# State transitions and state steps of a chunked RWKV-7 mixer, per pair of heads or per head

## The chip, the cores and the metric

The kernel runs on one core of a Trainium2 chip. The metric is device time in microseconds (us) of one execution; the time before is the median of three runs. TensorE does the matrix products (each as a load of weights, "PEld", and a product, "PE"), VectorE (DVE) and ScalarE (ACT) move and combine tiles, GpSimd (POOL) does some elementwise work and gathers, and SyncE (SP) issues most DMAs. An fp32 product of this kernel appears in the trace as two loads and two products.

## The reference, cut to what matters

Two layers, each a mixer (RWKV-7 time mixing beside a pooling mixer) and a PEER expert feed-forward. 512 tokens, width 1024, 8 RWKV heads of 64. The part that the change touches is the recurrence of each head, whose state is a 64 by 64 matrix:

```python
def rwkv7_step(state, inp):
    r_t, w_t, k_t, v_t, kk_t, a_t = inp
    sa = jnp.einsum('bhvk,bhk->bhv', state, -kk_t)
    state = (state * w_t[:, :, None, :]
             + sa[..., None] * (kk_t * a_t)[:, :, None, :]
             + v_t[..., None] * k_t[:, :, None, :])
    y = jnp.einsum('bhvk,bhk->bhv', state, r_t)
    return state, y
```

## The kernel before, in words

The mixer cuts the 512 tokens into 16 chunks of 32 (`CH`) and works on four pairs of heads per layer. Inside a pair the two heads lie one above the other on the 128 partitions (`hrs[0]` is rows 0 to 63, `hrs[1]` rows 64 to 127). Within a chunk everything is made by products; from chunk to chunk a state `M` of 128 x 64 (both heads) is carried: `M(c+1) = diag(P_c) M(c) + G_c^T M(c) + H_c`.

For each pair a list of blocks is written out: scaled and transposed copies, Gram matrices (`gram`, L625 and L628), `wu` (products L644, copies L646 and L572 on ScalarE), `hmat(0)`, `gmat`, `hmat(1)` and two `ypart`. `gmat` makes the 16 transitions: for each of 4 groups of 128 tokens and each of the 4 chunks in it one product of 32 rows and 128 columns (L662), into four PSUM banks, one per chunk position. Since both heads are in one product, the two off-diagonal 64 x 64 blocks mix the heads and are wrong; VectorE copies each bank (128 x 512) out and multiplies it with the mask `bones` of two diagonal blocks (L665). `hmat` (L674, copied by ScalarE at L678) makes the additive parts, in products of 64 x 64.

`chain(c)` is a state step: one product of 128 x 128 with the 64 columns of `M` (L706) into the single bank of the pool `psc`, and two operations of VectorE on 128 x 64: `M * P + H` (L707) and the sum with the product (L708). Step c needs `M` of step c-1. Step 0 is a copy, so there are 14 products per pair, 112 in all. `yout` (L717) applies the states in 64 x 64 products and `gn1`, `gn2` (L724 to L745) normalise.

The lists of different pairs are zipped: the later blocks of pair p go with the steps of pair p-1, the first blocks of pair p+2, the `adaLN` projections (DMA `raw<-ada`, VectorE L195 and L197) and, later, fills of the output projection (L277). The framework then orders each engine's instructions in a plan of its own, which follows the order of the program as a priority and its own estimate of when operands, tiles and banks are ready. Every engine runs its list in order. PSUM has eight banks: five in pool `ps`, two in `pss`, one in `psc`; a bank is taken again when its reader is done. SBUF tiles of 128 x 512 come from one pool, `s2`, of 38 slots.

Of the kernel before, what the change touches and what calls it, by code (L numbers as in the profile page):

```python
# [14 lines left out]
AF = mybir.ActivationFunctionType  # L15
ALU = mybir.AluOpType
# [3 lines left out]
P = 128  # L20
T = 512
NT = T // P
# [3 lines left out]
CH = 32  # L26
# [82 lines left out]
def body(ctx, tc, A, tap=None):  # L109
    nc = tc.nc  # L110
    V, S, G, TE = nc.vector, nc.scalar, nc.gpsimd, nc.tensor
# [11 lines left out]
    def nm(p):  # L123
        cnt[0] += 1
        return f"{p}{cnt[0]}"
# [6 lines left out]
    def sbank(shape=(P, T)):  # L132
        return pss.tile(list(shape), F32, tag="pss", name=nm("pss"))

    def s2t(name, shape=(P, T), dt=F32):
        return s2.tile(list(shape), dt, tag="s2", name=nm(name))
# [12 lines left out]
    def C(n):  # L149
        o, w = COFF[n]  # L150
        return const[:, o:o + w]
# [166 lines left out]
    def mixer(l):  # L318
        with ExitStack() as mctx:
# [126 lines left out]
            for p in range(4):  # L446
# [7 lines left out]
                for h in range(2):  # L454
                    hd = 2 * p + h
                    for cc in range(4):
                        rows = slice(cc * CH, (cc + 1) * CH)
# [4 lines left out]
                if p % 2 == 1:  # L462
                    for cc in range(4):
                        rows = slice(cc * CH, (cc + 1) * CH)
# [103 lines left out]
            def bank2(shape=(P, T)):  # L568
                nb[0] += 1
                return sbank(shape) if nb[0] % 4 == 0 and not apart[0] else psp[0].tile(list(shape), F32, tag="ps", name=nm("ps"))  # L570
# [4 lines left out]
            def pair(p):  # L575
                at, bt, kt, rt, v = at_[p], bt_[p], kt_[p], rt_[p], v_[p]
                hrs = [slice(h * 64, (h + 1) * 64) for h in range(2)]
                q3 = lambda n: s2t(n, (P, NT, P))
                z = {}
# [74 lines left out]
                def W(t):  # L654
                    return z["WU", t // 2][:, t % 2].rearrange("p h c -> p (h c)")[:, 64:192]

                def gmat():
                    pgs = [bank2((P, NT, P)) for _ in range(4)]
                    for t in range(NT):
                        for cc in range(4):  # L660
                            rows = slice(cc * CH, (cc + 1) * CH)
                            TE.matmul(pgs[cc][:, t], W(t)[rows], z["bk", cc % 2][rows, t], start=True, stop=True, tile_position=(cc * CH, 0))  # L662
                    for cc in range(4):
                        z["G", cc] = q3("G")
                        V.tensor_tensor(z["G", cc], pgs[cc], C("bones").unsqueeze(1).to_broadcast([P, NT, P]), op=ALU.mult)  # L665

                def hmat(s):
                    def f():
# [12 lines left out]
                def ypart(h):  # L681
                    def f():
# [3 lines left out]
                        for t in range(NT):  # L686
# [6 lines left out]
                blocks = [scaled(0, bt), scaled(1, kt), swapped, transposed("vT", v), gram("ak", kt, at, "lt"),  # L693
                          transposed("AX", at), transposed("UV", None), transposed(("bk", 0), None), transposed(("bk", 1), None), xm(0), xm(1),
                          gram("rb", bt, rt, "le"), gram("rkm", kt, rt, "le"), wu(0), wu(1), hmat(0), gmat, hmat(1), ypart(0), ypart(1)]

                def chain(c):
                    def f():
                        if c == 0:
                            z["M"] = [s2t("M", (P, 8, 64)) for _ in range(2)]  # L700
                            S.activation(z["M"][0][:, 1], z["H", 0][:, 0, 0], AF.Copy)
                            return
                        M = lambda i: z["M"][i // 8][:, i % 8]
                        hc = z["H", (c % 4) // 2][:, c % 2, c // 4]
                        pm = psc.tile([P, 64], F32, tag="psc", name=nm("psc"))
                        TE.matmul(pm, z["G", c % 4][:, c // 4], M(c), start=True, stop=True)  # L706
                        V.scalar_tensor_tensor(hc, M(c), PC[:, p, c:c + 1], hc, op0=ALU.mult, op1=ALU.add)  # L707
                        V.tensor_tensor(M(c + 1), hc, pm, op=ALU.add)  # L708
                    return f
# [605 lines left out]
```

## Time and profile before

| | us |
|---|---|
| median of 3 runs | 3448.68 |
| lowest and highest of these | 3448.21, 3457.46 |
| profiled execution, its own time | 3438.13 |
| its span, first to last instruction | 3436.4 |

Views of a profile give start and duration in us from the start of the span. "Idle before" an instruction is followed by an arrow to what ended the wait. In a table of stretches each engine has its busy time and, in brackets, its number of instructions; PEclk is the granted clock of TensorE as a share of 2.4 GHz.

### The profile page before, as it was taken

The numbers are of one execution on the slowest core, as the hardware profiler recorded it, in microseconds if no ns is written. First come the engines' busy times: TensorE is split into PE (matmuls) and PEld (weight loads), VectorE is DVE, ScalarE is ACT, GpSimd is POOL, SyncE is SP. The second block draws the span as 40 slices with busy tenths as digits, with TensorE's granted clock in tenths as the row PEclk, the third lists the DMA queues.
The fourth block names the chain that finished last, engine by engine and source line by source line (L and its number), as shares of the span: only waits on it lengthen the run. The fifth ranks groups of instructions, "written<-read, shape, count | busy, mean of one in ns | idle before, by whom it ended". The sixth has DMA issues, their size and how long they took to land. (4 is left out here: it accounts for less than half of the span.)

```text
span 3436.4 us, 51106 instructions
## 1 busy us (share of the span) xinstructions
PE 3211.2 (93%) x18154; PEld 2814.1 (82%) x18154; DVE 2809.3 (82%) x6227; ACT 1386.0 (40%) x2228; POOL 875.7 (25%) x684
## 2 busy tenths in 40 slices
PE   5889888999999999999899898999999999999997
PEld 3777678999998888888777777889999888888886
DVE  5677499989868888899939675999997688888998
ACT  3433222446563334333353323334656533333333
POOL 2000001432202222555500000023240122245564
PEclk7989899999999999999999888999999999999998
DMA  5214253567789999999922233345767999999996
GB/s 196 77 47 144 88 176 122 171 228 257 262 310 344 345 343 342 350 377 398 356 72 82 79 111 117 99 134 180 275 237 282 333 334 343 342 340 335 362 392 237
DMA packets 361377, 826.41 MB, mean 240 GB/s; under 512 B 46496, under 2 KB 189600, under 8 KB 357792
## 3 DMA queue, kind: packets, MB, share of 16 engines
q1 hardware_dynamic: 287392, 554.68, 47.5%
q0 software_dynamic: 73728, 268.47, 20.8%
q8 instruction: 142, 2.33, 0.3%
q14 instruction: 115, 0.94, 0.1%
HBM read 730.75 MB, written 92.27 MB: 240 GB/s over the span
## 5 line engine op out<-in xcount | busy, mean ns | idle before, releaser
L277 PE MATMUL pss<-hi,wsp 128*128 128x384 f32 (+1 forms) x5168 | 1081.5, 360 | 88.4 <-DVE wsp L260 27.8
L1162 PE MATMUL ps<-vv,wg 128*128 128x512 f32 x4608 | 1077.3, 392 | 22.7 <-DVE vv L1146 6.9
L277 PEld LDWEIGHTS pss<-hi,wsp 128*128 128x128 f32 x5168 | 941.0, 195 | 162.8 <-DVE wsp L260 39.9
L1162 PEld LDWEIGHTS ps<-vv,wg 128*128 128x128 f32 x4608 | 866.0, 189 | 208.0 <-ACT vv L1145 10.4
L259 ACT ACTIVATE wsp<-raw 128x1024 fp32r<-128x1024 f32 x341 | 360.0, 1057 | 548.5 <-PE pss L277 428.9
L277 PE MATMUL pss<-lo,wsp 128*128 128x384 f32 (+1 forms) x2584 | 534.1, 347 | 0.0
L855 POOL DMA_INDIRECT row<-u,ex x256 | 318.8, 1245 | 837.1 <-DVE row L861 639.5
L260 DVE TENSOR_TENSOR wsp<-raw,wsp 128x1024 fp32r<-128x1024 f32 x341 | 432.4, 1269 | 69.9 <-ACT wsp L259 69.7
L277 PEld LDWEIGHTS pss<-lo,wsp 128*128 128x128 f32 x2584 | 461.4, 188 | 22.2 <-issue 0.5
L855 POOL DMA_INDIRECT row<-v,ex x256 | 336.3, 1314 | 244.5 <-DVE ox L869 190.6
L1146 DVE TENSOR_TENSOR vv<-raw,vv 128x512 fp32r<-128x512 f32 x512 | 345.4, 692 | 43.1 <-ACT vv L1145 39.3
L1145 ACT ACTIVATE vv<-raw 128x512 fp32r<-128x512 f32 x512 | 291.4, 619 | 111.5 <-DMA raw<-v 76.9
L1136 ACT ACTIVATE wg<-ge 128x384 fp32r<-128x384 f32 x256 | 132.9, 524 | 497.6 <-DVE ge L1134 206.3
L861 DVE SCALAR_TENSOR_TENSOR row<-row,hx 128x1024 f32<-128x1024 f32 x256 | 318.4, 1250 | 14.0 <-DMA row<-u,ex 14.0
L869 DVE SCALAR_TENSOR_TENSOR ox<-row,wx,ox 128x1024 f32<-128x1024 f32 x254 | 325.3, 1281 | 2.4
L971 POOL TENSOR_TENSOR eq<-eq,cid 128x400 f32<-128x400 f32 x128 | 181.7, 1439 | 478.8 <-DVE eq L969 341.1
L937 POOL TENSOR_TENSOR hf<-hi,lo 128x128 f32<-128x128 f32 x16 | 7.8, 503 | 925.6 <-DVE tw L906 450.4
L1137 DVE TENSOR_TENSOR wg<-ge,wg 128x384 fp32r<-128x384 f32 x256 | 141.3, 555 | 104.6 <-ACT wg L1136 93.9
L1046 ACT ACTIVATE gb<-ps 128x512 f32<-128x512 f32 x192 | 199.0, 1161 | 0.0
L1134 DVE TENSOR_TENSOR ge<-ge,g 128x192 f32<-128x192 f32 x496 | 157.0, 353 | 46.3 <-DMA g<-gscr 39.3
L1129 ACT ACTIVATE ge<-pss 128x384 f32<-128x384 f32 x80 | 39.2, 490 | 249.0 <-PE pss L277 243.1
L1025 DVE TENSOR_TENSOR oh<-oh,selg 128x1024 f16<-128x1024 f16 x96 | 71.2, 742 | 44.9 <-PE ps L1044 44.7
(459 smaller groups left out, 3194.5 us busy)
## 6 DMA issues: line engine op xcount, KB each, us to landing
raw<-uT SPq DMA_DIRECT2D x256, 512.0 KB
raw<-v SPq DMA_DIRECT2D x256, 512.0 KB
gscr<-gb SPq DMA_DIRECT2D x24, 2048.0 KB
g<-gscr SPq DMA_DIRECT2D x124, 384.0 KB
gespill<-ge SPq DMA_DIRECT2D x176, 192.0 KB
ge<-gespill SPq DMA_DIRECT2D x176, 192.0 KB
ada<-ada SPq DMA_DIRECT2D x96, 256.0 KB
raw<-ada SPq DMA_DIRECT2D x48, 512.0 KB
```

What stands on the lines that cost most here:

```text
L259: S.activation(w[:, 0], raw, AF.Copy)
L260: V.tensor_tensor(w[:, 1], raw, w[:, 0].bitcast(F32), op=ALU.subtract)
L277: TE.matmul(pt, w[:, a, k * P:(k + 1) * P], hs[k][b], start=start and n == 0, stop=stop and n == len(steps) - 1)
L855: G.indirect_dma_start(out=rows[n], out_offset=None, in_=A["u" if n < P else "v"], in_offset=bass.IndirectOffsetOnAxis(ap=ex[:, n % P:n % ...
L861: V.scalar_tensor_tensor(row, row, 1.0, hx, op0=ALU.mult, op1=ALU.mult, accum_out=dots[:, e:e + 1])
L869: V.scalar_tensor_tensor(ox, row, wx[:, e:e + 1], ox, op0=ALU.mult, op1=ALU.add)
L971: pace["G"] = G.tensor_tensor(eq, eq, z["id"][:, h].unsqueeze(1).to_broadcast([P, 8, NC]), op=ALU.mult)
L1046: S.activation(gb[:, :, o:o + 4].rearrange("p i t -> p t i"), pt, AF.Copy, scale=1.0 / GSC)
L1134: V.tensor_tensor(gq, gq, g[:, :, c % IG], op=ALU.mult)
L1145: S.activation(vv[0][q], raw[:, q * T:(q + 1) * T], AF.Copy)
L1146: vlo[q] = V.tensor_tensor(vv[1][q], raw[:, q * T:(q + 1) * T], vv[0][q].bitcast(F32), op=ALU.subtract)
L1162: end[0] = TE.matmul(acc[t][d2], wg[a][:, ts_], vv[b][d2], start=(c == 0 and a == 0 and b == 0), stop=(c == NK - 1 and a == 1))
```

## The change

The transitions are made per head: 32 products of 32 rows and 64 columns per pair instead of 16 of 128 columns, each head into its own half of the partitions. The result holds no block that mixes heads, so there is no mask: ScalarE copies 128 x 256 out of each bank where VectorE multiplied 128 x 512, and two tiles hold what four held. A state step takes two products of 64 rows and 64 columns, one per head, into the two halves of the same bank.

```diff
                 def gmat():
-                    pgs = [bank2((P, NT, P)) for _ in range(4)]
+                    pgs = [bank2((P, NT, 64)) for _ in range(4)]
                     for t in range(NT):
                         for cc in range(4):
                             rows = slice(cc * CH, (cc + 1) * CH)
-                            TE.matmul(pgs[cc][:, t], W(t)[rows], z["bk", cc % 2][rows, t], start=True, stop=True, tile_position=(cc * CH, 0))
+                            for h in range(2):
+                                TE.matmul(pgs[cc][hrs[h], t], W(t)[rows, hrs[h]], z["bk", cc % 2][rows, t, hrs[h]], start=True, stop=True, tile_position=(cc * CH, h * 64))
                     for cc in range(4):
-                        z["G", cc] = q3("G")
-                        V.tensor_tensor(z["G", cc], pgs[cc], C("bones").unsqueeze(1).to_broadcast([P, NT, P]), op=ALU.mult)
+                        if cc % 2 == 0:
+                            z["G", cc // 2] = s2t("G", (P, 2, NT, 64))
+                        S.activation(z["G", cc // 2][:, cc % 2], pgs[cc], AF.Copy)
...
-                        TE.matmul(pm, z["G", c % 4][:, c // 4], M(c), start=True, stop=True)
+                        for h in range(2):
+                            TE.matmul(pm[hrs[h]], z["G", (c % 4) // 2][hrs[h], c % 2, c // 4], M(c)[hrs[h]], start=True, stop=True)
```

## Rows read from the trace of the kernel before

**Rows 1.** The page's first lines: span, and busy time of each engine.
```profile
span 3436.4 us, 51106 instructions
PE 3211.2 (93%) x18154; PEld 2814.1 (82%) x18154; DVE 2809.3 (82%) x6227; ACT 1386.0 (40%) x2228; POOL 875.7 (25%) x684
```
**Rows 2.** Table of stretches, three in each layer's mixer: start:end, length, busy by engine, clock.
```profile
250.60:256.00 5.40, 4.46 (x17) 3.50 (x16) 3.60 (x11) 0.00 (x0) 0.00 (x0) 0.50 0.01 3
284.90:291.40 6.50, 5.25 (x19) 3.32 (x17) 4.95 (x14) 0.00 (x0) 0.00 (x0) 0.64 0.00 1
329.10:336.60 7.50, 6.00 (x29) 4.53 (x28) 5.69 (x16) 0.63 (x1) 0.00 (x0) 0.86 0.00 0
...
1947.60:1953.00 5.40, 4.46 (x17) 3.50 (x16) 3.58 (x11) 0.00 (x0) 0.00 (x0) 0.50 0.00 0
1987.50:1993.20 5.70, 4.51 (x22) 2.79 (x15) 4.70 (x13) 0.00 (x0) 0.00 (x0) 0.71 0.00 1
2029.70:2037.00 7.30, 5.75 (x27) 3.99 (x26) 5.64 (x17) 0.63 (x1) 0.00 (x0) 0.82 0.01 2
```
**Rows 3.** Timeline of the second of these stretches, TensorE and then VectorE.
```profile
284.94 0.43 PE L706 MATMUL psc<-M,G 128*128 128x64 f32 x2
288.24 0.69 PE L706 MATMUL psc<-M,G 128*128 128x64 f32 x2 [0.31 <-DVE M L708]
290.53 1.06 PE L602 MATMUL pss<-const,bk 128*128 128x128 f32 x4
...
288.50 0.68 DVE L665 TENSOR_TENSOR G<-ps,const 128x512 f32<-128x512 f32 x1
290.49 0.68 DVE L665 TENSOR_TENSOR G<-pss,const 128x512 f32<-128x512 f32 x1
```
**Rows 4.** Timeline of ScalarE around the first layer's stretches.
```profile
256.18 1.08 ACT L613 ACTIVATE UV<-ps 128x512 f32<-128x512 f32 x2 [6.24 <-PE ps L602]
292.59 0.63 ACT L727 ACTIVATE sq<-y 128x512 f32<-128x512 f32 x1 [9.19 <-DVE y L725]
333.88 0.63 ACT L727 ACTIVATE sq<-y 128x512 f32<-128x512 f32 x1 [9.73 <-DVE y L725]
```
**Rows 5.** Instructions by line, whole span: duration in ns as min/median/max.
```profile
L665 DVE TENSOR_TENSOR G<-ps,const x26: 679/681/693, 230.3 to 2033.8; 128x512 f32<-128x512 f32 x26
L678 ACT ACTIVATE H<-ps x28: 378/383/418, 231.2 to 2039.6; 128x256 f32<-128x256 f32 x28
L706 PEld LDWEIGHTS psc<-M,G x224: 186/189/338, 238.9 to 2074.3; 128*128 128x128 f32 x112
```
**Rows 6.** Timeline of TensorE: weight loads of state steps and of 64 x 64 products.
```profile
342.30 0.30 PEld L706 LDWEIGHTS psc<-M,G 128*128 128x128 f32 x2
342.52 0.30 PEld L687 LDWEIGHTS ps<-rb,WU 128*128 128x128 f32 x2
346.94 1.36 PEld L717 LDWEIGHTS ps<-rt,M 64*64 64x64 f32 x44
348.35 0.30 PEld L706 LDWEIGHTS psc<-M,G 128*128 128x128 f32 x2
348.71 0.54 PEld L717 LDWEIGHTS ps<-rt,M 64*64 64x64 f32 x16
320.29 0.33 PEld L674 LDWEIGHTS ps<-UV,('bk', 0)439_2249 64*64 64x64 f32 x16
246.49 0.74 PEld L662 LDWEIGHTS ps<-('bk', 0)263_1492,WU 32*128 32x128 f32 x8 [0.17 <-issue]
```
**Rows 7.** Timeline: first and last of the 112 state steps, weight loads.
```profile
238.95 0.30 PEld L706 LDWEIGHTS psc<-M,G 128*128 128x128 f32 x2
...
2074.22 0.30 PEld L706 LDWEIGHTS psc<-M,G 128*128 128x128 f32 x2 [0.19 <-DVE M L708]
```
**Rows 8.** Timeline of ScalarE behind the first pair's `gmat`, first layer.
```profile
231.23 0.66 ACT L678 ACTIVATE H<-ps 128x256 f32<-128x256 f32 x2
232.42 0.38 ACT L678 ACTIVATE H<-pss 128x256 f32<-128x256 f32 x1 [0.53 <-PE pss L674]
```

## The prediction

> **What bounds the kernel now.** I read the page's head first. TensorE has something in flight for 93% of the span and its weight loads for 82%; VectorE is busy 82%, ScalarE 40% [rows 1]. So work taken from VectorE is worth nothing by itself: it pays only where TensorE stood still for it. The diff touches two short places, the two mixers (about 220 to 400 us and 1920 to 2100 us), so I cut these into stretches. Three stretches in each layer stand out [rows 2]: ScalarE is idle, VectorE half busy, the granted clock at 0.50 to 0.86, and TensorE holds only 15 to 28 weight loads in 5 to 8 us. Their lengths add up to 5.4 + 6.5 + 7.5 + 5.4 + 5.7 + 7.3 = 37.8 us, and weight loads run in 3.50 + 3.32 + 4.53 + 3.50 + 2.79 + 3.99 = 21.6 us of it.
>
> The timeline of one of them says why [rows 3]. From 284.94 to 288.24 us TensorE does nothing but five state steps one behind the other, each waiting for VectorE's L708 of the step before. The four transition banks had been written just before. VectorE takes them out only from 288.50 to 291.2 us, because its list holds the steps first and it waits inside each of them for TensorE. Until then four of seven banks are full, and the transposes of the next pair (L602) begin in earnest at 290.53. ScalarE stands idle meanwhile, for 6.24, 9.19 and 9.73 us in the first layer's three stretches [rows 4]. So the stretches are a hold: banks wait for a mask, the mask waits behind a chain, and TensorE has only the chain to run.
>
> **The change part by part.** *The copy.* It removes 32 masks (four per pair, eight pairs) of 0.681 us from VectorE, 21.8 us, and adds 32 copies of 128 x 256 from PSUM to ScalarE; the same shape costs 0.383 us at L678 [rows 5], 12.3 us in all. Neither sum is on the path. What is on it is when the banks come free. On ScalarE, idle in these stretches [rows 4], four copies take 4 x 0.383 = 1.5 us and can start as soon as the products are done: in the stretch of [rows 3] they would end near 286.5 instead of 291.2 us. Then transposes, `hmat(1)` and `ypart` fill the gaps between the steps. What can be gained is the time without a weight load, 37.8 - 21.6 = 16.2 us for both layers. I take four fifths, 13 us, since at the head of each stretch a step or two still stands alone. Lower bound: nothing, if the copies come late too. Upper bound: all 16.2, and more if the clock holds: weighted by their lengths it is 0.69 in these stretches [rows 2], and a third of 21.6 us of loads is another 7, so 23 us.
>
> *The steps.* A step's two loads occupy TensorE for 0.22 us in a stream (342.30 to 342.52). Four loads of 64 x 64 on two quarters are shown by `yout`: 44 loads in 1.36 us, that is (1.36 - 0.14) / 43 = 0.028 us each, 0.11 us for a step [rows 6]. So 0.11 us less for each of 112 steps [rows 7]. Some 28 of them lie in the stretches counted above; 84 x 0.11 = 9.2 us remain. `yout` streams 32 columns per product and a step 64, but the loads set the pace in that row. Bounds: nothing, if the two heads don't overlap, and 12.3 us, if all 112 count.
>
> *Changes of shape.* A step that goes from products of 128 rows to `yout`'s quarters starts the next load 0.36 us after its own first one (348.35 to 348.71), against 0.22 us in one shape: 0.14 us for a change [rows 6]. I counted the neighbours of the steps over the timeline between the first and the last [rows 7]. There are 80 uninterrupted groups of steps. 41 begin behind, and 42 end before, products that use a part of the array: 83 changes now. As quarters, steps fit with `yout` and `hmat` (18 of the beginnings, 31 of the ends) and change against all others: 62 + 49 = 111. The difference, 28 x 0.14 = 3.9 us, is lost. Bounds: none, if the order shifts kindly, and 224 - 83 = 141 changes, 19.7 us, if every step comes to stand alone among full products.
>
> *The transition products.* 256 loads of 32 x 128 become 512 of 32 x 64. Before, eight loads on two row groups took 0.74 us, (0.74 - 0.19) / 7 = 0.079 us each; small products on four quarters took (0.33 - 0.14) / 15 = 0.013 us each at L674 [rows 6]. No row shows 32 x 64. Bounds: 512 x 0.028 - 256 x 0.028 = 7 us lost, if each load costs the same whatever its width, and 256 x 0.079 - 512 x 0.013 = 13.6 us gained. I take nothing: half the columns, twice the loads, the same array.
>
> *The first pair of each layer* has no such hold: VectorE was free there, and ScalarE copies `H` from 231.23 and again at 232.42 us [rows 8]. The new copies queue behind the first, delay the second by up to 1.5 us, and keep `hmat(1)`'s successors waiting for banks. I charge 1 us per layer, 2 us (bounds 0 and 3.1). The two saved tiles of `s2` per pair I count as nothing: no wait that I read was for a slot, and adaLN and the copies have slots now; if that cover is gone, it can only help. DMA stays as it is: its share was 0.01 or less in the stretches [rows 2].
>
> *Sum* against the profiled execution of 3438.13 us: -13 - 9.2 + 3.9 + 0 + 2 = -16.3 us. That execution lies 10.5 us under the median of the runs, 3448.68 us; nothing in the sum depends on this, so I carry the difference over: 3432 us.
>
> **The rule that speaks against it.** `yout`'s loads run at 0.028 us though its two heads, rows 0 to 63 and rows 64 to 127, write two halves of one bank [rows 6], just as the new steps do. The Trainium skill, TensorEngine Tiling (Array Packing), section Restrictions and Gotchas, says that different row tiles cannot access the same PSUM bank simultaneously. By that rule the heads of a step would take turns; this trace does not agree. The rival below needs no more than the mechanism.
>
> **Rivals.** *The hold stays* (chance 0.20). ScalarE's list is in order too. In two of the three stretches its next instruction waits for VectorE's `y` (L725) [rows 4]. If the plan puts the copies behind it, or if TensorE's list still holds the steps in a row, the 13 us don't come: -9.2 + 3.9 + 2 = -3.3 us, 3445 us, no measurable change. Against it: the copies stand earlier in the program than those normalisations, and their operands are ready earlier.
>
> *The heads take turns* at the bank (0.05). Four loads of half the columns one after the other cost what two of all columns cost, 0.22 us; the 9.2 us are lost, -7.1 us, 3442 us, still within the measurement. For it is only that no row shows 64 columns per quarter; against it stands the row of `yout`.
>
> *Changes of shape outweigh the rest* (0.13), the slower side. If the hold goes, steps are spread among other products, 128 wide most of them, and each pays 0.14 us on either side. With the 13 us intact it would need (13 + 9.2 - 2) / 0.14 = 144 added changes, as many as there can be. With the hold in place it needs (9.2 - 2) / 0.14 = 51 to reach no change and about 125 to pass 0.3%. At 141 added changes and no relief: 19.7 + 2 - 9.2 = 12.5 us more, 3461 us.
>
> **How the numbers follow.** My forecast, the hold dissolved, has 0.62: 3432 us, and by its own bounds (-23 - 9.2 - 4 for a kind order and narrower transitions, to -4 where a quarter of the hold's gain comes) 3412 to 3444. A measurement of this kernel tells about 0.3%, 10 us, from no change, so faster means under 3438. The forecast's case falls there in nearly all its weight, and the measured fate of the rivals gives: faster 0.62, same 0.27 (both middle rivals and the forecast's weak end), slower 0.11. The range reaches to the two middle rivals and to no change: 3412 to 3450.
>
> **What would show it.** Right: in each mixer the L665 rows of VectorE are gone and ScalarE copies `G` within 2 us of the last L662; groups of four or five steps with waits of 0.31 us shrink to one or two; the three stretches get shorter by 2 us each and their clock rises; a step's loads take 0.11 us in a stream. Wrong: the G copies start late, behind an instruction of ScalarE that waits; or the steps' loads are 0.05 us apart and not overlapped; or gaps of 0.3 us before and after single steps add up to more than 10 us. The prediction falls too if the time saved in the mixers returns as a longer wait for VectorE or for adaLN's DMA before the feed-forward.

## The result, and the profile after

The changed kernel takes 3418.26 us (median of 8 runs, 3415.88 to 3425.93) against 3443.37 us (8 runs, 3433.64 to 3457.46): ratio 0.9928 [0.9912, 0.9945], some 25 us. (Five more runs have lowered the median before from the 3448.68 us that the forecast counted from.) The same pair measured again gave 0.9890 [0.9858, 0.9923], 38 us. Its profiled execution took 3418.91 us. The page's first lines, which answer to [rows 1]:

```profile
span 3417.1 us, 52040 instructions
...
PE 3187.3 (93%) x18634; PEld 2786.5 (82%) x18634; DVE 2787.6 (82%) x6195; ACT 1396.2 (41%) x2260; POOL 867.6 (25%) x684
```

The gain lies in the two mixers. The table of stretches, each mixer from its first `wu` product (L644) to its first update of `x` (L794 before, L797 after), first of the kernel before and then of the changed one (columns as in [rows 2]: busy us and counts of TensorE's products, its weight loads, VectorE, ScalarE, GpSimd; granted clock; DMA share; GB/s):

```profile
225.29:392.48 167.19, 153.15 (x1345) 126.62 (x1344) 107.14 (x255) 50.84 (x115) 0.00 (x0) 0.83 0.26 83
1922.10:2089.05 166.95, 151.13 (x1345) 124.75 (x1344) 107.27 (x255) 50.84 (x115) 0.00 (x0) 0.86 0.26 83
sum 334.14, PE 304.29 PEld 251.37 DVE 214.41 ACT 101.67 POOL 0.00; mean PE 152.14 PEld 125.68 DVE 107.21 ACT 50.84 POOL 0.00
```

```profile
226.32:379.82 153.50, 139.31 (x1585) 112.16 (x1584) 97.03 (x238) 55.48 (x130) 0.00 (x0) 0.88 0.29 90
1916.01:2068.83 152.82, 139.58 (x1585) 111.12 (x1584) 97.18 (x238) 55.42 (x130) 0.00 (x0) 0.87 0.29 91
sum 306.32, PE 278.88 PEld 223.28 DVE 194.21 ACT 110.90 POOL 0.00; mean PE 139.44 PEld 111.64 DVE 97.10 ACT 55.45 POOL 0.00
```

Both mixers together shrink from 334.1 to 306.3 us, 27.8 us, and the weight loads in them from 251.4 to 223.3 us, 28.1 us. The time without a weight load is 334.1 - 251.4 = 82.8 us before and 306.3 - 223.3 = 83.0 us after. So TensorE saves what it loads, and the time without a load comes out the same. That speaks against my largest term, which was a wait; but the same total can hide one wait that grew and one that shrank, and the experiments show that it does.

Outside the mixers the changed kernel's profile is 8.5 us longer (spans less mixers: 3102.3 and 3110.8 us). Two profiles of the kernel before differ there by 15 us (3102.3 and 3117.3), so this shows no loss.

The same stretches behind `gmat` as in [rows 2], each from the last transition products to the first stream of `hmat` or `ypart` behind the transposes, in the changed kernel:

```profile
249.60:252.21 2.61, 1.95 (x21) 1.45 (x21) 2.35 (x8) 1.19 (x4) 0.00 (x0) 1.00 0.00 0
283.20:286.59 3.39, 2.74 (x39) 1.57 (x22) 3.09 (x11) 1.21 (x4) 0.00 (x0) 1.00 0.00 0
324.40:328.90 4.50, 3.65 (x58) 2.47 (x54) 2.60 (x9) 1.40 (x4) 0.00 (x0) 0.95 0.00 0
1939.30:1941.89 2.59, 1.94 (x20) 1.43 (x21) 2.32 (x9) 1.17 (x4) 0.00 (x0) 1.00 0.01 3
1970.70:1973.31 2.61, 2.29 (x19) 1.32 (x18) 2.50 (x8) 1.20 (x4) 0.00 (x0) 1.00 0.00 0
2014.60:2019.35 4.75, 3.90 (x54) 2.73 (x55) 2.84 (x9) 1.39 (x4) 0.00 (x0) 0.86 0.00 0
sum 20.45, PE 16.47 PEld 10.97 DVE 15.69 ACT 7.56 POOL 0.00; mean PE 2.74 PEld 1.83 DVE 2.62 ACT 1.26 POOL 0.00
```

They have shrunk from 37.8 to 20.5 us, by 17.3, of which 6.7 us are time without a load (16.2 to 9.5 us), and the clock in them has risen from 0.50 to 0.86 up to 0.86 to 1.00. (The clock is that of one profile. In the changed kernel's second one the first stretch, from 253.33 to 256.81 us, takes 3.5 us at a clock of 0.72.) Seen by themselves these rows seem to confirm the hold. What ended the first stretch shows in the timelines of pair 1, layer 0. First the kernel before, weight loads and VectorE's first mask:

```profile
250.68 0.50 PEld L706 LDWEIGHTS psc<-M,G 128*128 128x128 f32 x2 [0.22 <-issue]
...
251.68 0.50 PEld L706 LDWEIGHTS psc<-M,G 128*128 128x128 f32 x2 [0.50 <-DVE M L708]
...
252.68 0.50 PEld L706 LDWEIGHTS psc<-M,G 128*128 128x128 f32 x2 [0.50 <-DVE M L708]
...
253.68 0.50 PEld L706 LDWEIGHTS psc<-M,G 128*128 128x128 f32 x2 [0.50 <-DVE M L708]
...
253.95 0.68 DVE L665 TENSOR_TENSOR G<-ps,const 128x512 f32<-128x512 f32 x1
253.95 0.87 PEld L602 LDWEIGHTS pss<-const,bk 128*128 128x128 f32 x4
```

And the changed kernel, ScalarE's copies and weight loads, with the products of one step:

```profile
249.58 0.38 ACT L667 ACTIVATE G<-ps 128x256 f32<-128x256 f32 x1
...
249.61 0.20 PEld L709 LDWEIGHTS psc<-M,G 64*64 64x64 f32 x4 [0.17 <-DVE M L711]
...
249.86 0.38 ACT L667 ACTIVATE G<-pss 128x256 f32<-128x256 f32 x1
...
250.12 0.67 ACT L667 ACTIVATE G<-ps 128x256 f32<-128x256 f32 x2
...
250.26 0.20 PEld L709 LDWEIGHTS psc<-M,G 64*64 64x64 f32 x4 [0.46 <-DVE M L711]
250.27 0.33 PE L709 MATMUL psc<-M,G 64*64 64x64 f32 x4 [0.33 <-DVE M L711]
...
250.92 0.20 PEld L709 LDWEIGHTS psc<-M,G 64*64 64x64 f32 x4 [0.46 <-DVE M L711]
...
251.18 0.42 PEld L602 LDWEIGHTS pss<-const,bk 128*128 128x128 f32 x4
```

Before, the transposes (L602) load at 253.95, 0.27 us behind the last step's load and in the same moment in which the *first* mask begins; no bank of `G` had come free. After, they load at 251.18, again 0.26 us behind the last step. Layer 1 shows the same 0.27 us in both kernels. TensorE's list has four steps of the pair before there (the first of them, after, between the last transition products, at 248.95), and the transposes come next in the list. (Why the plan puts four steps there, and whether it reckons with the banks, no run shows; it did so in every kernel below.) The stretch is so many steps times the period of a step: 1.00 us before, at a clock of 0.50, and 0.655 us after. At the full clock the period before was 0.75 us, in the stretch of [rows 3]:

```profile
285.69 0.30 PEld L706 LDWEIGHTS psc<-M,G 128*128 128x128 f32 x2 [0.45 <-DVE M L708]
...
286.44 0.30 PEld L706 LDWEIGHTS psc<-M,G 128*128 128x128 f32 x2 [0.45 <-DVE M L708]
```

In pair 2 the mean product of the pair before stands between the steps and the transposes, from 288.62 to 289.68 us before and from 284.84 to 285.38 after: the same work at the two levels of the clock.

The steps' weight loads over the whole span, before and after (busy us, mean ns, idle time just before them and what ended it):

```profile
L706 PEld LDWEIGHTS psc<-M,G 128*128 128x128 f32 x224 | 40.3, 220 | 32.5 <-DVE M L708 27.4 <-issue 0.9
```

```profile
L709 PEld LDWEIGHTS psc<-M,G 64*64 64x64 f32 x448 | 24.5, 143 | 32.8 <-DVE M L711 20.0 <-issue 5.0 <-DVE H L710 3.6
```

40.3 us have become 24.5, 15.8 less, while the idle time in front comes out the same (32.5 and 32.8 us). In all fourteen profiles of this document these loads take 38.8 to 41.3 us where the steps are full and 24.3 to 25.8 us where they are narrow. A step's period is its loads plus a wait for VectorE that does not depend on the width: 0.30 + 0.45 = 0.75 us before at full clock, 0.20 + 0.46 = 0.66 us after. The transition products' weight loads in the two mixers (length of the mixers, busy us; mean of one mixer), L662 before and L663 after:

```profile
sum 334.14, PEld 18.30; mean PEld 9.15
```

```profile
sum 306.32, PEld 11.27; mean PEld 5.64
```

Another 7.0 us; 17.9 to 20.5 us with full transitions and 11.1 to 11.4 us with narrow ones in the fourteen profiles. The rest lies in lines that the change does not touch, counted in the same way (loads of different lines can overlap, so the lines do not add up to the whole): the transposes L602 12.4 to 9.2 us, the variance products 12.8 to 10.4, `ypart` 48.6 to 44.3, `yout` 20.1 to 21.1. These are as many loads of the same shapes as before; the granted clock of the two mixers rose from 0.83 and 0.86 to 0.88 and 0.87.

### The profile page after: what moved, and what is told of

It reads as the page before. It is cut to its first block, busy times and chain, and to the rows that moved or that the text cites. A ratio compares the mean times of both kernels' runs of the same rounds, so it can differ in the third digit from the quotient of the medians.

```text
span 3417.1 us, 52040 instructions
## 1 busy us (share of the span) xinstructions
PE 3187.3 (93%) x18634; PEld 2786.5 (82%) x18634; DVE 2787.6 (82%) x6195; ACT 1396.2 (41%) x2260; POOL 867.6 (25%) x684
## 5 line engine op out<-in xcount | busy, mean ns | idle before, releaser
L1165 PEld LDWEIGHTS ps<-vv,wg 128*128 128x128 f32 x4608 | 867.0, 189 | 210.6 <-ACT vv L1148 17.9
```

Source lines behind the costliest of these rows:

```text
L1165: end[0] = TE.matmul(acc[t][d2], wg[a][:, ts_], vv[b][d2], start=(c == 0 and a == 0 and b == 0), stop=(c == NK - 1 and a == 1))
```

## Experiments

All are timed against the kernel before on the same chip. Theory at the outset: the hold of the banks gives most, and the copy on ScalarE alone would show it; rival: the narrower products give most. "Loads" is the weight loads' busy time in both mixers, "rest" the mixers without them, "low" the time at 1.2 GHz, worked out as 2 x (1 - granted clock) x length for each mixer. The edits are shown shortened: `bones` and `hsel` are constants of zeros and ones, without their indexing.

| kernel | ratio | clock of the timed runs | mixers, us | loads | rest | low |
|---|---|---|---|---|---|---|
| before | 1 | 0.9510 to 0.9517 | 334.1 | 251.4 | 82.8 | 104 |
| before, again | (one run) | 0.952 | 336.2 | 251.9 | 84.4 | 111 |
| copy alone (ScalarE masks) | 1.0021 [1.0004, 1.0037] | 0.9492 | 340.1 | 260.9 | 79.2 | 129 |
| copy alone, split | 1.0006 [0.9984, 1.0029] | 0.9500 | 334.4 | 255.4 | 79.0 | 111 |
| steps alone | 0.9944 [0.9918, 0.9971] | 0.9545 | 330.2 | 237.7 | 92.5 | 103 |
| transitions alone | 0.9979 [0.9957, 1.0002] | 0.9508 | 336.8 | 250.8 | 86.0 | 118 |
| both narrow, VectorE copies | 0.9941 [0.9918, 0.9963] | 0.9545 | 318.4 | 231.3 | 87.2 | 102 |
| full transitions | 0.9944 [0.9925, 0.9963] | 0.9533 | 317.9 | 237.0 | 80.9 | 95 |
| full steps | 0.9955 [0.9939, 0.9971] | 0.9526 | 318.7 | 244.4 | 74.4 | 99 |
| changed | 0.9928 [0.9912, 0.9945] | 0.9556 | 306.3 | 223.3 | 83.0 | 77 |
| changed, again | 0.9890 [0.9858, 0.9923] | 0.9557 | 308.7 | 225.8 | 82.9 | 80 |
| changed, copies split | 0.9920 [0.9890, 0.9951] | 0.9545 | 309.2 | 226.4 | 82.8 | 87 |
| changed, warm tail | 0.9931 [0.9908, 0.9954] | 0.9575 | 303.4 | 225.0 | 78.4 | 64 |
| before, filled | 1.0058 [1.0035, 1.0081] | 0.9500 | 347.1 | 261.7 | 85.5 | 108 |

**The copy alone.** Full transitions and full steps; ScalarE takes out the banks and masks on the way, by a factor 0 or 1 for each row.

```diff
-V.tensor_tensor(z["G", cc], pgs[cc], bones, op=ALU.mult)
+for h in range(2):
+    S.activation(z["G", cc][:, :, hrs[h]], pgs[cc][:, :, hrs[h]], AF.Copy, scale=C("hsel")[:, h:h + 1])
```

> Only the engine of the mask changes: transitions and steps stay full, ScalarE makes the block diagonal from each bank with two copies of 128 x 256, each scaled by a column of ones and zeros (8 x about 0.4 = 3.2 us per pair, where the change needs 4 x 0.39). From the first product of wu to the first update of x, before took 167.6 and 167.3 us in the two layers and after 153.9 and 153.2: 27.8 us less, of which 25 show in the time. Theory H (the hold: banks wait for a mask that waits behind the chain on VectorE): most of the prediction's 13 us come from this alone, the two mixers 10 to 13 us shorter, groups of steps behind gmat shorter. Theory N (narrower products, in steps and transitions, give it all, since time without a weight load is the same 83 us before and after): under 4 us.

Measured: 7 us slower [1, 13]. ScalarE's copies and the weight loads in pair 1, layer 0:

```profile
254.52 0.84 ACT L666 ACTIVATE G<-ps,const 128x256 f32<-128x256 f32 x2
...
255.25 0.84 ACT L666 ACTIVATE G<-pss,const 128x256 f32<-128x256 f32 x2
...
255.38 0.50 PEld L707 LDWEIGHTS psc<-M,G 128*128 128x128 f32 x2 [0.50 <-DVE M L709]
...
255.96 1.59 ACT L666 ACTIVATE G<-ps,const 128x256 f32<-128x256 f32 x4
...
256.38 0.50 PEld L707 LDWEIGHTS psc<-M,G 128*128 128x128 f32 x2 [0.50 <-DVE M L709]
...
257.38 0.50 PEld L707 LDWEIGHTS psc<-M,G 128*128 128x128 f32 x2 [0.50 <-DVE M L709]
...
257.65 0.87 PEld L602 LDWEIGHTS pss<-const,bk 128*128 128x128 f32 x4
```

The first bank is free at 255.36, the second at 256.09, and still the transposes load only at 257.65, 0.27 us behind the last step. So no bank held them, here or before. The theory of the hold falls, for the transposes that it was made for.

**The copy split.** Two of four banks are masked by ScalarE as above, two by VectorE as before.

```diff
+if cc % 2:
+    for h in range(2):
+        S.activation(z["G", cc][:, :, hrs[h]], pgs[cc][:, :, hrs[h]], AF.Copy, scale=C("hsel")[:, h:h + 1])
+    continue
 V.tensor_tensor(z["G", cc], pgs[cc], bones, op=ALU.mult)
```

> The kernel before with full transitions and full steps, but the second and the fourth bank of a pair's transitions are masked by ScalarE (two half copies each, scaled by 0 or 1 per row) and the first and the third by VectorE as before: so ScalarE's extra work is half that of the run in which it did all the masking (12 us in place of 24 in the two mixers), and all four banks come free sooner. If the hold of the banks by itself sets the stretches behind the transitions, as the prediction had it (13 us for six stretches shortened by 4.5 us each): shortened by 1.5 to 3 us each, 4 to 9 us faster, ratio 0.997 to 0.999, and the run with all masking on ScalarE failed by its eight copies a pair. If the hold is worth something only where the steps and transitions behind it are narrow: no gain, ratio 1.000 to 1.002, mixers 334 to 340 us.

Measured: no difference (1.0006 [0.9984, 1.0029]), mixers 334.4 us. With half of the copies on ScalarE no loss is to be seen, and a gain still does not appear.

**The steps alone.** Two 64 x 64 products read the diagonal quarters of the masked blocks.

```diff
-TE.matmul(pm, z["G", c % 4][:, c // 4], M(c), start=True, stop=True)
+for h in range(2):
+    TE.matmul(pm[hrs[h]], z["G", c % 4][hrs[h], c // 4, hrs[h]], M(c)[hrs[h]], start=True, stop=True)
```

> Only the step is changed against the kernel before: the transitions are still made whole and masked by VectorE into full 128x128 blocks, and the two 64x64 products of a step read the diagonal quarters of those blocks. Theory A, that a narrower step pays by itself wherever it stands: between the two worths that the runs so far showed for it in the mixers (22 us with whole transitions, 12 us with quarter transitions, both with copies by ScalarE), so 12 to 22 us, about 3428 us, ratio 0.995. Theory B, that the parts only pay together, since the stretches behind gmat are held by VectorE's masking as long as it is there: what is left of the change's 28 us when 12 for the engine and 12 for the transitions are taken off, about 4 us, 3441 us, ratio 0.999. By both the hold behind gmat stays: the last masking of pairs 1 and 2 ends 5 to 6 us after the last product of the transitions.

Measured: 19 us faster [10, 28], as theory A had it. The steps' weight loads:

```profile
L707 PEld LDWEIGHTS psc<-M,G 64*64 64x64 f32 x448 | 25.1, 145 | 38.1 <-DVE M L709 25.7 <-issue 4.2 <-PE ps L725 2.3
```

25.1 us in place of 40.3, with VectorE's masking untouched. Its profile has only 4 us of the gain in the mixers: loads fell by 13.7 us, while the waits in front of the steps rose by 5.6 us, and the first mixer ran 10 us longer than the second, at a clock of 0.81 against 0.88. So a single profile places a gain of this size badly, and the timed runs decide.

**The transitions alone.** `gmat` as after the change; VectorE spreads each half bank over a full block with the mask, one instruction for each bank as before.

```diff
+for h in range(2):
+    TE.matmul(pgs[cc][hrs[h], t], W(t)[rows, hrs[h]], z["bk", cc % 2][rows, t, hrs[h]], ..., tile_position=(cc * CH, h * 64))
...
+V.tensor_tensor(z["G", cc], pgs[cc] repeated for both halves, bones, op=ALU.mult)
```

> Only the transition products are changed against the kernel before: they are made per head, on quarters, into 64 columns; VectorE then spreads each half bank over a full 128x128 block with the mask, in one instruction per bank, and the steps take the whole block as before. Theory A, that narrower transition products pay by themselves: 12 to 21 us, about 3428 us, ratio 0.995. Theory B, that the parts only pay together: about 3 us, 3442 us, ratio 0.999. The price set down in the prediction for this part by itself was nothing, between a loss of 7 and a gain of 13.6 us. Banks: still four, each held until its masking is done, 5 to 6 us behind the last product in pairs 1 and 2.

Measured: 7 us faster [1 slower to 15 faster by the interval], unclear. It lies between the two theories.

**One part taken back.** Three kernels each undo one part of the change: VectorE copies in place of ScalarE; full transitions (ScalarE takes the diagonal quarters in eight copies a pair); full steps (ScalarE builds the full blocks in eight copies a pair).

```diff
-S.activation(z["G", cc // 2][:, cc % 2], pgs[cc], AF.Copy)
+V.tensor_copy(z["G", cc // 2][:, cc % 2], pgs[cc])
```

```diff
-S.activation(z["G", cc // 2][:, cc % 2], pgs[cc], AF.Copy)
+for h in range(2):   # pgs as before: (P, NT, P)
+    S.activation(z["G", cc // 2][hrs[h], cc % 2], pgs[cc][hrs[h], :, hrs[h]], AF.Copy)
```

```diff
-S.activation(z["G", cc // 2][:, cc % 2], pgs[cc], AF.Copy)
+for h in range(2):   # steps as before, on G of (P, NT, P)
+    S.activation(z["G", cc][:, :, hrs[h]], pgs[cc], AF.Copy, scale=C("hsel")[:, h:h + 1])
```

> All of the change but the engine: transitions and steps per head, but VectorE copies the 128 x 256 banks (about 0.38 us each, without a mask). Theory H: the hold stays, since VectorE's list is in order, so only the shorter steps come, 5 us (9.2 less 3.9 for changes of shape). Theory N: 20 to 28 us as in the whole change.

> Transitions made full, 16 products of 128 columns per pair as before; ScalarE copies the two diagonal blocks out (two copies of 64 partitions per bank, 8 per pair), steps per head. Differs from the whole change by the shape of the transition products and four more copies per pair. The prediction counted nothing for that shape: by it, within 3 us of the whole change (two mixers 24 to 28 us shorter). Theory N, with weight loads of gmat busy for 18.3 us before and 11.3 after: 7 us or more of the gain are missing here.

> Steps full, one product of 128 x 128 as before; transitions per head, and ScalarE lays each bank into the block diagonal with two copies of 128 x 256 scaled by a column of ones and zeros (8 per pair). Differs from the whole change by the shape of the steps and four more copies per pair. The prediction's terms: the steps are worth 9.2 - 3.9 = 5 us, so two mixers 20 to 23 us shorter. Theory N, with weight loads of the steps busy for 40.3 us before and 24.5 after: 16 us of the gain are missing, 8 to 12 us shorter.

Measured: 20, 19 and 15 us faster than before, against 25 and 38 us with all parts; by the ratios each part taken back costs 4 to 9 us against the changed kernel's first measurement, no more than about its error, and 18 to 22 us against its second. Theory N is the nearer for the first two; the mixers of the third, 15 us shorter, lie between the theories. Alone, the steps bring 19 us, the transitions 7 and the copy -7; any two of them 15 to 20 us; all three 25 to 38 us. Sums and differences of these are uncertain by some 10 us. The steps bring 9 to 26 us in every setting; that the parts do not add stands clear of the error only for transitions and copy, whose worths alone sum to 0, against 15 us together.

*What the equal totals hide.* Four pairs of kernels differ in the engine that empties the banks (with two copies a bank in the first three). Idle time in front of the steps' loads, and the mixers without loads, with VectorE and then with ScalarE, us:

| the rest of the kernel | idle before steps | rest | by the timed ratios |
|---|---|---|---|
| all full | 32.5 to 28.2 | 82.8 to 79.2 | 7 slower |
| steps narrow | 38.1 to 30.4 | 92.5 to 80.9 | 0 |
| transitions narrow | 30.3 to 24.6 | 86.0 to 74.4 | 8 faster |
| both narrow | 34.3 to 32.8 | 87.2 to 83.0 | 5 to 18 faster |

So ScalarE takes something off TensorE's waits each time, and narrow steps, whose loads are shorter, wait longer in front of them. The two cancel in the 82.8 and 83.0 us. With everything full, what ScalarE takes off the waits is lost again in loads at a lower clock (251.4 to 260.9 us). Each of these numbers is from one profile; two profiles of one kernel differ by 0.4 and 0.7 us in the idle time before the steps. One place where VectorE's masks hold TensorE is in pair 3 of the kernel before, by VectorE's own list and not by a bank:

```profile
330.41 1.88 DVE L665 TENSOR_TENSOR G<-ps,const 128x512 f32<-128x512 f32 x3
...
332.40 0.68 DVE L665 TENSOR_TENSOR G<-ps,const 128x512 f32<-128x512 f32 x1
...
333.00 0.21 DVE L708 TENSOR_TENSOR M<-H,psc 128x64 f32<-128x64 f32 x1
...
333.26 0.30 PEld L706 LDWEIGHTS psc<-M,G 128*128 128x128 f32 x2 [0.97 <-DVE M L708]
```

Four masks stand in front of the step's sum, and the next step waits 0.97 us where it waits 0.45 otherwise. How much of the table is of this kind is not shown.

**The same kernels again**, for what one profile is worth.

> The changed kernel once more, on the chip of the two runs beside it, with a second profile: ratio 0.993 again, and its two mixers together within 4 us of the 306.3 us of its first profile if the differences of 12 us between variants are not the scatter of single profiles. Its mean granted clock over the runs 0.955 to 0.956, that of the kernel before beside it 0.951 to 0.952.

> The kernel before once more, for a second profile of it: the two mixers together within 4 us of 334.1 us if single profiles can be compared at that grain; if they scatter by 10 us or more, the differences of 12 us between the variants' profiles say little by themselves, and only the timed ratios count.

Measured: mixers 308.7 us against 306.3, and 336.2 against 334.1. That is less than the 12 us between variants, from one more profile of either kernel, and with the reserve that the steps alone and the split copy (174.1 and 160.3 us for its two mixers) impose.

**Copies split in the changed kernel**: first and third on ScalarE, second and fourth on VectorE.

```diff
-S.activation(z["G", cc // 2][:, cc % 2], pgs[cc], AF.Copy)
+(acopy, V.tensor_copy)[cc % 2](z["G", cc // 2][:, cc % 2], pgs[cc])
```

> The changed kernel with the second and the fourth copy of a pair's transitions on VectorE, the first and the third on ScalarE. If the time to the release of the banks is what the engine is worth (1.2 us behind the last product with ScalarE alone, 3.2 to 3.4 with VectorE alone, 12 us between the two in the mixers): the two engines side by side release no later, and the mixers stay at 306 to 309 us or gain up to 5, 3412 to 3418 us. If it is VectorE's own queue, out of which the copies are taken: half of the 12 us comes back, mixers 312 to 315 us, 3424 us, ratio 0.994 against the kernel before.

Measured: 0.9920, mixers 309.2 us, no different from the changed kernel, as the first theory had it, but not for its reason: the banks came free later, not sooner: the last copies of pairs 1 and 2 ended 2.5 and 3.2 us behind the last product, against 1.2 us with ScalarE alone. So no cost of a later release, or of half of the copies on VectorE, is to be seen here.

**Filling the stretch behind the transitions of the kernel before** with products that nobody reads, into the steps' bank, to see whether the clock alone would give the gain.

```diff
+if p in (1, 2):
+    for i in range(4):
+        TE.matmul(pf[:, 64:T], C("bones"), WU[:, 64:T], start=True, stop=True)
```

> The kernel before with four extra products of 128x128 by 128x448 right behind the transition products of pairs 1 and 2, into the steps' bank, which nobody reads: TensorE waits 5 to 6 us for banks there, and nothing else of the kernel is changed. Clock theory, that the short waits behind the transitions let the clock fall and that half of the change's gain was this: the time at the lower level in the two mixers falls from 99 to 104 us towards the 68 to 78 us of the changed kernel, worth up to 0.46 x 28 = 13 us, 3433 us, ratio 0.996, without any of the change's work. Work theory, that the gain came from loads and holds alone: 0 to 3 us slower for each of the four places, 3446 to 3458 us, ratio 1.000 to 1.003.

Measured: 20 us slower [12, 28]. TensorE in pair 1, layer 0, steps, transposes and the added products:

```profile
257.19 0.69 PE L711 MATMUL psc<-M,G 128*128 128x64 f32 x2 [0.31 <-DVE M L713]
257.67 1.06 PE L602 MATMUL pss<-const,bk 128*128 128x128 f32 x4
...
262.01 3.17 PE L669 MATMUL psc<-WU,const 128*128 128x448 f32 x8
```

The added products did not land in the waits: their place in TensorE's list is 8 us behind the transitions, between full products, and each of the four groups takes 3.17 us of it. 4 x 3.17 = 12.7 us, and the mixers are 13 us longer (347.1 against 334.1). So this says nothing about the clock, but it says that TensorE's list is the bound in these places: a microsecond put into it makes the mixers about a microsecond longer.

**A warm tail.** The changed kernel with five unread products in the group norm of each layer's last pair.

```diff
+warm(2)   # behind the mean product, for the last pair only
...
+warm(1)   # behind the variance product
...
+warm(2)   # behind the last scale product
```

> The changed kernel with five extra products of 128x128 by 128x512 in the group norm of each layer's last pair (two behind the mean product, one behind the variance product, two behind the last scale product), into a bank that nobody reads: they fill waits of TensorE of 1.0 to 3.4 us at the end of the mixer and change no value. Clock theory, by the slope over the 128 timed runs so far (3.1 us for each 0.001 of mean granted clock, about 0.46 us for each us at the lower level): the lowered stretch of some 10 us that ends each mixer goes, in two layers 20 us, 9 us faster than the changed kernel, about 3408 us, mean clock 0.958 to 0.959. Work theory: the tail of the mixer is a chain of single instructions, so a higher clock gives nothing there, and the five products cost 0 to 4 us in each layer where they stand in the way: 3418 to 3426 us.

Measured: 0.9931, 3418.52 us, no different from the changed kernel. From the last step's sum to the first update of `x`, changed kernel and then this one:

```profile
364.70:379.82 15.12, 9.83 (x34) 6.57 (x33) 4.65 (x8) 2.15 (x4) 0.00 (x0) 0.66 0.00 1
2053.00:2068.83 15.83, 10.54 (x36) 7.23 (x33) 4.68 (x8) 2.15 (x4) 0.00 (x0) 0.58 0.00 1
```

```profile
370.97:383.47 12.50, 10.69 (x45) 6.00 (x43) 4.67 (x8) 2.15 (x4) 0.00 (x0) 1.00 0.00 1
2055.70:2068.12 12.42, 10.61 (x43) 6.00 (x43) 4.64 (x8) 2.15 (x4) 0.00 (x0) 1.00 0.00 0
```

The clock there rose from 0.66 and 0.58 to 1.00, and the two tails are 2.6 and 3.4 us shorter: even a chain of single instructions goes faster. Half of these 6 us is gone within the mixers: the stretch in front of the tail, from the first `wu` product on, took 3.0 us longer in layer 0 (138.38 to 141.40 us) and the same in layer 1. In the timed runs nothing of the rest is to be seen, although their mean clock rose from 0.9556 to 0.9575. The time is in the range of the work theory, though its reason, that a higher clock gives nothing in such a chain, is not what the profile shows; why the mixer of layer 0 took longer, and where the other 3 us went, stays open.

## Why the prediction was right, and where it was not

The sign, the place and the range were right: 3412 to 3450 us forecast, 3418.26 and 3412.12 us measured. The sum was -16.3 us; measured are -25 and -38. The largest term came from a mechanism that the runs refute, and terms that were too small made up for it: that the time came near the forecast is in good part luck.

*The copy* (-13 us) failed, and by its reading, not its size. [Rows 3] show steps one behind the other and masks behind them, and I took the masks for what holds the transposes. The row that decides was in the same timeline of the stretch before: L602 loads 0.27 us behind the last step, when the first mask has only begun. TensorE's list holds the steps in a row; that was in the prediction, as the rival "the hold stays", with 0.20. The sign to look for came true for another reason: ScalarE's copies end 1.2 us behind the last product, the stretches are shorter by 2.5 to 3.1 us each and their clock is higher, but groups of three steps with waits of 0.46 us in front of their loads remain, where one or two steps were forecast. The copy alone is worth nothing in the timed runs (1.0021, 1.0006). With both products narrow, ScalarE in place of VectorE takes the ratio from 0.9941 to 0.9928 and 0.9890, 5 to 18 us, from separate measurements and with intervals that overlap. The profiles agree with such a gain, by shorter waits in front of the steps; how VectorE's list and the plan share in it, when half of the copies on VectorE cost nothing, stays open.

*The steps* (-9.2 us) were too small, and are the main term: 15.8 us of weight loads over all 112, not 84, steps, 19 us [10, 28] in the run with the steps alone. I had left 28 steps out as counted in the hold, and took the loads at full clock. At that clock 112 x (0.30 - 0.20) = 11 us; the rest is that many steps ran at 1.2 GHz before, 0.50 us for the loads (250.68 above), and fewer do now. In a stream the 0.11 us came true, among the 64 x 64 products of `hmat` (weight loads):

```profile
252.62 0.18 PEld L709 LDWEIGHTS psc<-M,G 64*64 64x64 f32 x2
252.67 0.13 PEld L676 LDWEIGHTS ps<-UV,('bk', 1)265_1499 64*64 64x64 f32 x1
...
252.68 0.18 PEld L709 LDWEIGHTS psc<-M,G 64*64 64x64 f32 x2
...
252.73 0.43 PEld L676 LDWEIGHTS ps<-UV,('bk', 1)265_1499 64*64 64x64 f32 x10
```

From 252.62 to 252.73 it is 0.11 us, with a load of `hmat` among them.

*The transition products* (0) were too small: 7.0 us of loads, near the middle of the gain that I had bounded by 13.6. *Changes of shape* (+3.9 us) were 50 more, not 28 (186 to 236 from one load to the next in the two mixers), 7 us at my price of 0.14. Whether they cost that is not shown: the rest, 82.8 and 83.0 us, holds them together with waits that changed. *The first pair* (+2 us) was 0: counted from the first `wu` product, which came 1.0 us later in this profile, the second copy of `H` starts after 7.5 instead of 7.1 us (233.87 and 232.42 in the two spans), not 1.5 us later, and the next pair's `wu` starts 14.8 us after the first pair's, against 15.1 before.

*The clock* was not in the sum, only in a bound. Take half of the low time off the mixers in the table, an estimate as if all work went half as fast then: 282 and 281 us before, 268 and 269 us after, 279 for the steps alone, 278 for the transitions alone, 276 for the copy alone, 267 to 270 with any two parts. So about 13 us are saved at equal clock, and any two parts save all of it; with the third the low time falls from 95 to 102 us to 77 and 80. Over all 192 timed runs of these kernels, each against the mean of its own kernel and chip, 0.001 of mean clock (6.9 us at 1.2 GHz) goes with 3.1 us of time (standard error 0.2). The changed kernel's mean is 0.004 to 0.005 higher: 12 to 15 us of its gain go along with that. That this is cause and not only company is not shown: the warm tail raised the clock without a gain in the timed runs, and the filled kernel did not test it. Why the clock falls less often with all three parts than with two stays open.

*The heads take turns* fell: a step's four loads take 0.20 us and its four products 0.33 us (250.26 and 250.27 above), where two full loads take 0.30 us [rows 6] and two full products 0.43 us at the same clock [rows 3], although both heads write two halves of one bank. The Trainium skill, TensorEngine Tiling (Array Packing), section Restrictions and Gotchas, would have them apart; this trace does not agree. *Changes of shape outweigh the rest* fell too.

## What to carry to other kernels

When a stretch is full of waits, ask what comes next in the waiting engine's own list, before asking which buffer is held: here the transposes of pair 1 followed the last step by 0.26 to 0.28 us in every kernel but one (0.40 us with the steps alone), whatever freed the banks. Where a busy engine works through a list, compare its busy time in the stretch before and after (251.4 to 223.3 us) and the rest (82.8 to 83.0 us); the first shows what a narrower product buys, the second only the sum of all changes of waits. An unchanged sum does not say that nothing changed: here it took kernels with one part each to see a longer wait and a shorter one cancel. So a part's worth is to be had by running it alone and by taking it back alone.

## What the runs showed of the hardware that I had not expected

Loads of 32 x 64 on eight tiles overlap far more than I had dared to assume: one lasts 0.13 us, but 512 of them, with eight tiles in use, keep the loader busy for 11.3 us in the mixers, 0.022 us each, where 256 of 32 x 128, with four tiles, took 18.3, 0.071 us each (at mixed clocks: 0.88 and 0.87 in the mixers with the first, 0.83 and 0.86 with the second). A single chain of dependent products goes faster at the higher clock as well: the tail of 15 to 16 us became 12.5. And the same kernel's profile can differ by 14 us from one mixer to the next with nearly the same list (174.1 and 160.3 us in the split copy), at clocks of 0.80 and 0.87.
